# Routing tiles 5 and 6 sorted one by one, weight loads moved ahead of the gather, the last output scattered in two halves

## The chip, the cores and the metric

The kernel runs on one core of a Trainium2 chip. The metric is the device time of one execution in microseconds. A core has five engines that work side by side, each through its own instructions in their order: TensorE (PE in the rows; PEld is its weight loading), VectorE (DVE), ScalarE (ACT), GpSimd (POOL) and SyncE (SP, which here only starts transfers). They wait for each other through semaphores. 16 DMA engines move data between HBM and the on-chip memory.

## The reference

One transformer block over 1024 tokens of width 1024: a modulated norm, an mLSTM mixer beside a dilated attention mixer, an output projection, and then a mixture of experts in which each of 16 experts chooses its 128 tokens. What the change touches is the last part:

```python
def expert_choice_ffn(h, w_router, b_router, w_gate, w_up, w_down):
    cap = (EC_CAPACITY_FACTOR * S) // N_EXPERTS          # 128
    affinity = jax.nn.softmax((h @ w_router + b_router), axis=-1)
    gates, idx = lax.top_k(affinity.transpose(0, 2, 1), cap)
    xin = h[bidx, idx]
    hid = silu(einsum('becd,edf->becf', xin, w_gate)) * einsum('becd,edf->becf', xin, w_up)
    y = einsum('becf,efd->becd', hid, w_down) * gates[..., None]
    return zeros_like(h).at[bidx, idx].add(y)
```

The result is x + gate2 times this. All arithmetic is in f32; the expert weights are 16 experts x 3 matrices of 1024 x 2048 floats, 403 MB.

## The kernel before

The tokens lie in 8 tiles of 128. Three stages matter here.

**The output projection** (`phase_out`) makes the residual stream x tile by tile. Tiles 0 to 2 come together; tiles 3 to 7 follow in a loop of 40 steps (5 tiles x 2 halves x 4 pieces of the contraction), and each step issues three matmuls of 512 columns. A half ends with an addition on VectorE that empties PSUM (line 1196) and a write of x to `out` in HBM. The norm of the tile (`out_norm`), its transposition and its router logits (`out_tail`, line 1150) follow some steps later.

**The routing** needs, for each expert, the 128th largest of 1024 affinities. `route_sort(i0, n)` does softmax for n tiles, transposes the affinities so that experts lie on partitions, takes the 64 largest of each half row in 8 rounds (MAX of eight values, then MATCH_REPLACE, which the trace shows as MATCH_VALUE_LOAD and MATCH_REPLACE8), sorts with a `bitonic` network of 7 levels of two instructions (lines 1285 and 1286), merges the n tiles, and merges the result into `self.best`, the running 128 largest, with 7 more levels. It is a generator: the loop of `phase_out` starts a sort at the steps of the table `SORTS` and lets `pump` advance the oldest sort by `PUMP` pieces in each step. Tiles 0 to 2 are one sort, tiles 3 and 4 one, tiles 5 and 6 one. Tile 7 is sorted in `route_select`, which then makes the threshold `thr` (line 1397), the mask, the slots and a one-hot matrix for expert 0. `route_expert` turns that into row numbers `idx`, and an indirect DMA on GpSimd's queue gathers the 128 rows into `xin` (line 1445).

**The experts** (`phase_experts`) run one after the other. Weights come in pieces of 1 MB into a ring of tiles; `feed` starts a load, `cut_high` makes the rounded part `wh` on ScalarE (line 1489), `cut` makes the rest `wl` on VectorE (line 1505) and feeds the tile again, and `mm` runs the 12 matmuls of a piece, the last four of them on `wl`. `expert_down` for expert e runs while expert e+1 is in work; it ends with two multiplications into `xin` (line 1580) and an indirect DMA that adds the 128 rows into `out` (line 1581), called the scatter here. All scatters add into the same `out`, and in the built program each waits for the scatter ahead of it to land. `idx` tiles come from a set of three buffers (`bufs=3`), so the fourth `idx` takes the buffer of the first when all that read it are done.

Ahead of the gather of expert 0 the first loads are started on SyncE's queue; the last three entries of the list `late` are started on GpSimd's queue behind the gather.

Of the kernel before, what the change touches and what calls it, by code (L numbers as in the profile page):

```python
# [14 lines left out]
I32 = mybir.dt.int32  # L15
AF = mybir.ActivationFunctionType
OP = mybir.AluOpType
# [3 lines left out]
P = 128  # L21
# [23 lines left out]
RING = 8  # L45
EARLY = 6
FEEDS = (2, 8, 14, 20, 26, 32)
LATE = 3
CUTS = 4
HT = (1, 3, 5, 7)  # L50
PAIR0 = 2, 4, 5
MIX = 8
SORTS = {9: (0, 3), 24: (3, 2), 39: (5, 2)}
PUMP = 2
G1 = 3
TAIL1 = 2, 2, 4
TAIL = 4, 6
# [49 lines left out]
class K:  # L107
# [1045 lines left out]
    def phase_out(self):  # L1153
        nc, I, tc, m1, mx = self.nc, self.I, self.tc, self.m1, self.mx
        psum = lambda: self.psm.tile([P, 512], F32, name="pm")
        self.h2_d = tc.dram_tile([S, D], F32, name="h2_d")
        ss = m1.tile([P, 2, NT], F32, name="ss2")
        with ExitStack() as st:
# [34 lines left out]
            def epilogue(i, c, ps):  # L1193

                x, t = X[i][:, c * 512:(c + 1) * 512], slice(c * 512, (c + 1) * 512)
                nc.vector.tensor_add(x, ps, x)
                sq = self.rp.tile([P, 512], BF16, name="sq2", tag="wo_raw", bufs=4)
                nc.scalar.activation(sq, x, AF.Square, accum_out=ss[:, c, i:i + 1])
                nc.sync.dma_start(out=self.out[i * P:(i + 1) * P, t], in_=x)
# [5 lines left out]
            last, spare = psum(), psum()  # L1205
# [23 lines left out]
            todo, side = {}, []  # L1229
            at = lambda n, g: todo.setdefault(n, []).append(g)  # L1230

            def pump(n):
                for _ in range(n):
                    if side and next(side[0], 1):
                        side.pop(0)

            def finish(i, rs, when):
                g = self.out_tail(i, X[i], rs)
                next(g)
                at(when[0], lambda: next(g))  # L1240
                at(when[1], lambda: next(g))
# [8 lines left out]
            for i in range(G1, NT):  # L1250
                for c in range(2):
                    ps = psum()
                    for k in range(MH):
                        mm(ps, i, c, k)
                        step += 1
                        for g in todo.pop(step, ()):
                            g()
                        if step in SORTS:
                            side.append(self.route_sort(*SORTS[step]))
                        if step in FEEDS:  # L1260
                            self.feed()
                        pump(PUMP)
                    epilogue(i, c, ps)
# [30 lines left out]
    def route_sort(self, i0, n, last=False):  # L1294

        nc, rt = self.nc, self.rt
        lg = self.lg[:, i0:i0 + n]
        aff = self.aff[:, i0:i0 + n, 0:NE]
        R = 32 * n
        mx = rt.tile([P, 4], F32, name="r_mx", bufs=2)[:, :n]  # L1300
        sm = rt.tile([P, 4], F32, name="r_sm", bufs=2)[:, :n]
        nc.vector.tensor_reduce(mx, lg, axis=AX.X, op=OP.max)
        nc.vector.tensor_sub(aff, lg, mx[:, :, None].to_broadcast([P, n, NE]))
        if n == 1:
            nc.scalar.activation(aff[:, 0], aff[:, 0], AF.Exp, accum_out=sm)
        else:
            nc.scalar.activation(aff, aff, AF.Exp)
        yield 0
        if n > 1:
            nc.vector.tensor_reduce(sm, aff, axis=AX.X, op=OP.add)  # L1310
        nc.vector.reciprocal(sm, sm)
        nc.vector.tensor_mul(aff, aff, sm[:, :, None].to_broadcast([P, n, NE]))
        ps = self.psm.tile([P, 512], F32, name="pm")
        nc.tensor.transpose(ps[:R, :P], self.aff[:, i0:i0 + n].rearrange("p s e -> p (s e)"), self.ident)

        w = next(self.r_work).rearrange("p (h t) -> p h t", h=2)
        a, b = next(self.bit_a), next(self.bit_b)
        if n > 2:
            y = self.rp.tile([P, P], F32, name="r_rows")
            nc.vector.tensor_copy(y[:R], ps[:R, :P])  # L1320
            yield 0
            t = self.rp.tile([P, 64], F32, name="r_top")
            src = y[:R].rearrange("p (h m) -> p h m", h=2)
            top = a[:R], t[:R]
            w = w[:R]
            for r in range(8):
                for h in range(2):
                    nc.vector.max(top[h][:, 8 * r:8 * r + 8], src[:, h])
                if r < 7:
                    for h in range(2):  # L1330
                        nc.vector.match_replace(w[:, h], top[h][:, 8 * r:8 * r + 8], src[:, h], -1.0)
                    src = w
                yield 0
            nc.vector.tensor_copy(a[:R, 64:], t[:R, ::-1])
        else:

            R2 = slice(0, 2 * R)
            x, w = w[R2, 0], w[R2, 1]
            for h in range(2):
                if last and h == 0:  # L1340
                    nc.vector.tensor_copy(x[h * R:(h + 1) * R], ps[:R, 64 * h:64 * h + 64])
                else:
                    nc.scalar.activation(x[h * R:(h + 1) * R], ps[:R, 64 * h:64 * h + 64], AF.Copy)
            yield 0
            for r in range(8):
                nc.vector.max(a[R2, 8 * r:8 * r + 8], x)
                if r < 7:
                    nc.vector.match_replace(w, a[R2, 8 * r:8 * r + 8], x, -1.0)
                    x = w
                yield 0  # L1350
            nc.vector.tensor_copy(a[:R, 64:], a[R:2 * R, 63::-1])
        yield from self.bitonic(a, b, slice(0, R))
        a, b = self.sorted
        while n > 1:
            R, m = 32 * ((n + 1) // 2), 32 * (n // 2)
            nc.vector.tensor_copy(b[:m], a[R:R + m, ::-1])
            nc.vector.tensor_max(b[:m], a[:m], b[:m])
            if m < R:
                nc.vector.tensor_copy(b[m:R], a[m:R])
            n = R // 32  # L1360
            yield 0
            yield from self.bitonic(b, a, slice(0, R))
            a, b = self.sorted
        if i0:
            nc.vector.tensor_max(b[:32], self.best[:32], a[:32, ::-1])
            if not last:
                yield from self.bitonic(b, a, slice(0, 32))
                a, b = self.sorted
            else:
                a = b  # L1370
        self.best = a
        yield 0
# [137 lines left out]
    def mm(self, xs, n, first, last):  # L1510

        nc = self.nc
        w, l = self.ready.pop(0)
        (xh, xl), ps = xs, n
        N = len(ps) * 512
        prods = (xh, w), (xl, w), (xh, l)
        order = [(q, t, c) for q in range(3) for t in range(FF // N) for c in range(len(ps))]
        if last and not (self.fed or self.halves or self.ready):

            order.sort(key=lambda a: (a[1], a[0], a[2]))  # L1520
        for q, t, c in order:
            x, y = prods[q]
            o = t * N + c * 512
            nc.tensor.matmul(ps[c], x[:, t], y[:, o:o + 512], start=first and q == 0 and t == 0, stop=last and (q, t) == (2, FF // N - 1))  # L1524
        if self.ahead:
            self.ahead -= 1
        else:
            self.cut()
# [36 lines left out]
        self.split(h, l, ps.rearrange("p (k n) -> p k n", k=4))  # L1565
        u.setdefault("hT", []).append((h, l))

    def expert_down(self, u, psum):

        nc = self.nc  # L1570
        ps = [psum() for _ in range(2)]
        for i in range(8):
            h, l = u["hT"][i // 2]
            k = slice(2 * (i % 2), 2 * (i % 2) + 2)
            self.mm((h[:, k], l[:, k]), ps, i == 0, i == 7)
            yield i
        y = self.xin
        for c in range(2):
            t = slice(c * 512, (c + 1) * 512)
            nc.vector.scalar_tensor_tensor(y[:, t], ps[c], u["gate"], self.gate2[:, t], op0=OP.mult, op1=OP.mult)  # L1580
        nc.gpsimd.indirect_dma_start(out=self.out, out_offset=bass.IndirectOffsetOnAxis(ap=u["idx"][:, :1], axis=0),  # L1581
                                     in_=y, in_offset=None, compute_op=OP.add)

    def phase_experts(self):


        nc = self.nc
# [5 lines left out]
        half = lambda pool, tag, **kw: pool.tile([P, D], F32, name="w_half", tag=tag, **kw)  # L1593
        og = lambda: half(self.yp, "og", bufs=MH)
# [2 lines left out]
        self.xin = self.m1.tile([P, D], F32, name="xin", bufs=2)  # L1597
        for _ in range(2):
            self.feed([half(self.yap, "ya", bufs=MH) for _ in range(2)], once=True)
        late = [None] * (RING - EARLY) + [[og(), og()], [og(), half(self.m2, "w_x")]]  # L1600
        for t in late[:-LATE]:
            self.feed(t)
        _, u = self.route_expert(0, sets[1])
        for t in late[-LATE:]:
            self.feed(t, nc.gpsimd)
        for _ in range(CUTS - 1):
            self.cut()
        for b in range(2):
# [4 lines left out]
        p = None  # L1613
        for e in range(NE):
            X, Y = sets[e % 2], sets[1 - e % 2]
            n = None
# [6 lines left out]
            for i in self.expert_up(u, "w_up", Y):  # L1623
# [3 lines left out]
                if e + 1 < NE and i == 2:  # L1627
                    n = next(route)
            for c in range(4):
                t = slice(c * 512, (c + 1) * 512)  # L1630
# [9 lines left out]
                    self.expert_xT(n, b, Y)  # L1640
            p, u = u, n
        self.expert_hT(p, 3, Y)
        for _ in self.expert_down(p, Y):
            pass


# [100 lines left out]
```

## Time and profile before

| | us |
|---|---|
| median of 3 runs | 1841.47 (1836.42 to 1842.91) |
| the profiled execution: time | 1833.95 |
| the profiled execution: span on the core | 1832.0 |
| TensorE busy in that span | 1722.9 (94%) |
| VectorE busy | 1487.1 (81%) |
| ScalarE busy | 1197.7 (65%) |
| time at which the last addition of the projection starts | 640.0 |
| time at which the first expert matmul starts | 679.4 |

Times in the rows below count from the start of the span. The profiled execution is one of its own, 7.5 us below the median of the three runs. Busy shares are means over stages with different limits, so the stages have to be read one by one.

### The profile page before, as it was taken

To read this page: it belongs to the slowest core of one execution; us is meant where nothing else is said; L and a number is where in the kernel's file an instruction comes from. 1 tells how busy PE (TensorE), PEld (TensorE's weight loads), DVE (VectorE), ACT (ScalarE), POOL (GpSimd) and SP (SyncE) were. 2 spreads that over 40 slices of the span, in tenths; PEclk is the share of its full clock that TensorE was granted. 3 is DMA by queue.
4 is the path that set the end of the run, shared out by engine and by line. 5 is a ranking of instruction groups with operands and counts; after the bars stand their busy time and mean duration, and the time that the engine had idled before them with its cause. 6 is when DMAs were issued, how large, how long until landed. Compare 5 with 4: busy or idle time off the path is not lost. (4 is left out here: it accounts for less than half of the span.)

```text
span 1832.0 us, 24429 instructions
## 1 busy us (share of the span) xinstructions
PE 1722.9 (94%) x8696; PEld 1402.8 (77%) x8696; DVE 1487.1 (81%) x2156; ACT 1197.7 (65%) x1603; POOL 180.5 (10%) x185
## 2 busy tenths in 40 slices
PE   5999999989998939999999999999999999999997
PEld 4777888778886827888888778777787777777785
DVE  5578885687866788988988898888898888888886
ACT  5346454377763537787777777776776776777764
POOL 1001000031123020010110000100000001001000
PEclk9999999999999959999999999999999999999999
DMA  9135663325557768999999999999999999999892
GB/s 325 42 114 172 213 215 98 110 80 116 135 129 227 258 255 336 359 354 382 410 363 345 373 345 379 372 335 390 352 369 384 357 364 387 329 382 368 311 391 67
DMA packets 152553, 517.26 MB, mean 282 GB/s; under 512 B 33163, under 2 KB 50833, under 8 KB 116721
## 3 DMA queue, kind: packets, MB, share of 16 engines
q1 hardware_dynamic: 138560, 478.92, 70.7%
q0 software_dynamic: 10960, 36.32, 7.5%
q8 instruction: 68, 1.11, 0.2%
q10 hardware_dynamic: 2912, 0.48, 0.2%
q14 instruction: 53, 0.43, 0.1%
HBM read 488.16 MB, written 27.50 MB: 281 GB/s over the span
## 5 line engine op out<-in xcount | busy, mean ns | idle before, releaser
L1505 DVE TENSOR_TENSOR wl<-w,wh 128x2048 fp32r<-128x2048 f32 x278 | 627.8, 2285 | 81.6 <-ACT wh L1489 81.2
L1489 ACT ACTIVATE wh<-w 128x2048 fp32r<-128x2048 f32 x278 | 523.1, 1919 | 55.2 <-PE py L1524 26.3
L1505 DVE TENSOR_TENSOR wl<-w_half,wh 128x1024 fp32r<-128x1024 f32 x210 | 245.6, 1217 | 8.6 <-ACT wh L1489 8.5
L1489 ACT ACTIVATE wh<-w_half 128x1024 fp32r<-128x1024 f32 x210 | 211.8, 1058 | 24.1 <-PE px L1524 13.1
L1524 PE MATMUL py<-wl,xTh 128*128 128x512 f32 x512 | 139.9, 394 | 7.7 <-DVE wl L1505 7.7
L1524 PE MATMUL px<-wl,xTh 128*128 128x512 f32 x512 | 139.7, 394 | 4.5 <-DVE wl L1505 4.5
L1524 PE MATMUL px<-wh,xTh 128*128 128x512 f32 x512 | 141.1, 395 | 2.3 <-ACT xTh L124 2.1
L1524 PE MATMUL py<-wh,xTh 128*128 128x512 f32 x512 | 140.8, 394 | 2.2 <-ACT wh L1489 2.0
L1524 PE MATMUL py<-wh,xTl 128*128 128x512 f32 x512 | 138.3, 390 | 0.0
L1524 PE MATMUL px<-wh,xTl 128*128 128x512 f32 x512 | 138.1, 391 | 0.0
L1524 PE MATMUL px<-wh,hT 128*128 128x512 f32 x512 | 130.4, 396 | 0.1
L1524 PE MATMUL py<-wh,hT 128*128 128x512 f32 x512 | 129.0, 393 | 0.0
L1524 PEld LDWEIGHTS py<-wl,xTh 128*128 128x128 f32 x512 | 94.6, 188 | 33.4 <-DVE wl L1505 14.6
L1524 PEld LDWEIGHTS px<-wl,xTh 128*128 128x128 f32 x512 | 95.0, 188 | 29.5 <-DVE wl L1505 10.4
L1524 PEld LDWEIGHTS px<-wh,xTh 128*128 128x128 f32 x512 | 95.3, 189 | 23.9 <-ACT xTh L124 2.5
L1524 PEld LDWEIGHTS py<-wh,xTh 128*128 128x128 f32 x512 | 94.7, 188 | 24.0 <-ACT wh L1489 4.5
L1524 PEld LDWEIGHTS px<-wh,hT 128*128 128x128 f32 x512 | 95.6, 190 | 22.1 <-ACT wh L1489 2.1
L1524 PEld LDWEIGHTS px<-wh,xTl 128*128 128x128 f32 x512 | 96.7, 189 | 20.6
L1524 PEld LDWEIGHTS py<-wh,xTl 128*128 128x128 f32 x512 | 96.0, 188 | 20.4 <-DVE xTl L125 0.2
L1524 PEld LDWEIGHTS py<-wh,hT 128*128 128x128 f32 x512 | 95.0, 188 | 20.8 <-ACT wh L1489 0.7
L1581 POOL DMA_INDIRECT out_dram<-xin,idx x16 | 48.3, 3019 | 590.6 <-DVE xin L1580 590.6
L1445 POOL DMA_INDIRECT xin<-h_d,idx x16 | 37.8, 2362 | 477.9 <-DVE rg L1443 197.4
(456 smaller groups left out, 3138.2 us busy)
## 6 DMA issues: line engine op xcount, KB each, us to landing
w<-in_w_down_dram SPq DMA_DIRECT2D x95, 1024.0 KB, 8.4
w<-in_w_gate_dram SPq DMA_DIRECT2D x91, 1024.0 KB, 7.2
w<-in_w_up_dram SPq DMA_DIRECT2D x88, 1024.0 KB, 7.1
w_half<-in_w_gate_dram SPq DMA_DIRECT2D x70, 512.0 KB, 7.6
w_half<-in_w_up_dram SPq DMA_DIRECT2D x70, 512.0 KB, 7.5
w_half<-in_w_down_dram SPq DMA_DIRECT2D x66, 512.0 KB, 8.3
ada_w<-in_w_ada_dram SPq DMA_DIRECT2D x64, 256.0 KB, 3.5
wraw<-in_w_in_dram SPq DMA_DIRECT2D x20, 512.0 KB, 4.3
```

What stands on the lines that cost most here:

```text
L1445: nc.gpsimd.indirect_dma_start(out=xin, out_offset=None, in_=self.h2_d, in_offset=bass.IndirectOffsetOnAxis(ap=idx[:, :1], axis=0))
L1489: act = self.nc.scalar.activation(h[:, j * m:(j + 1) * m], t, AF.Copy)
L1505: self.tc.keep_in_program_order(self.nc.vector.tensor_sub(l[:, c], t, h[:, c]))
L1524: nc.tensor.matmul(ps[c], x[:, t], y[:, o:o + 512], start=first and q == 0 and t == 0, stop=last and (q, t) == (2, FF // N - 1))
L1581: nc.gpsimd.indirect_dma_start(out=self.out, out_offset=bass.IndirectOffsetOnAxis(ap=u["idx"][:, :1], axis=0), in_=y, in_offset=None, comp ...
```

## The change

Four edits. (1) The sort of tiles 5 and 6 together at step 39 becomes a sort of tile 5 at step 31 and one of tile 6 at step 39; `pump` advances up to four pieces per step in place of two; and each sort but that of tile 7 yields 2 four times ahead of the transposition of its affinities, which ends the pumping of that step, so that the transposition comes four steps later in the program. (2) The three late pieces are fed on SyncE's queue ahead of the gather and no longer on GpSimd's behind it. (3) In the very last piece of weights the matmuls are ordered by output half first, so that half 0 is complete after six matmuls and half 1 after twelve. (4) The last expert's output is scattered in two indirect DMAs of half rows; each has row numbers of its own, 2 idx + half, made on VectorE in a tile `row` that is drawn from the `idx` buffers.

```diff
-LATE = 3
-SORTS = {9: (0, 3), 24: (3, 2), 39: (5, 2)}
-PUMP = 2
+SORTS = {9: (0, 3), 24: (3, 2), 31: (5, 1), 39: (6, 1)}
+PUMP = 4
+PAUSE = 4
...
             def pump(n):
                 for _ in range(n):
-                    if side and next(side[0], 1):
+                    r = next(side[0], 1) if side else 2
+                    if r == 1:
                         side.pop(0)
+                    if r == 2:
+                        break
...
         nc.vector.tensor_mul(aff, aff, sm[:, :, None].to_broadcast([P, n, NE]))
+        if not last:
+            for _ in range(PAUSE):
+                yield 2
         ps = self.psm.tile([P, 512], F32, name="pm")
...
         if last and not (self.fed or self.halves or self.ready):
 
-            order.sort(key=lambda a: (a[1], a[0], a[2]))
+            order.sort(key=lambda a: (a[2], a[0], a[1]))
...
-    def expert_down(self, u, psum):
+    def expert_down(self, u, psum, last=False):
...
             nc.vector.scalar_tensor_tensor(y[:, t], ps[c], u["gate"], self.gate2[:, t], op0=OP.mult, op1=OP.mult)
-        nc.gpsimd.indirect_dma_start(out=self.out, out_offset=bass.IndirectOffsetOnAxis(ap=u["idx"][:, :1], axis=0),
-                                     in_=y, in_offset=None, compute_op=OP.add)
+            if last:
+
+                row = self.rt.tile([P, 1], I32, name="idx", bufs=3)
+                nc.vector.tensor_scalar(row, u["idx"], 2.0, float(c), op0=OP.mult, op1=OP.add)
+                nc.gpsimd.indirect_dma_start(out=self.out.rearrange("s (h n) -> (s h) n", h=2), out_offset=bass.IndirectOffsetOnAxis(ap=row[:, :1], axis=0),
+                                             in_=y[:, t], in_offset=None, compute_op=OP.add)
+        if not last:
+            nc.gpsimd.indirect_dma_start(out=self.out, out_offset=bass.IndirectOffsetOnAxis(ap=u["idx"][:, :1], axis=0),
+                                         in_=y, in_offset=None, compute_op=OP.add)
...
-        late = [None] * (RING - EARLY) + [[og(), og()], [og(), half(self.m2, "w_x")]]
-        for t in late[:-LATE]:
+        rest = [None] * (RING - EARLY) + [[og(), og()], [og(), half(self.m2, "w_x")]]
+        for t in rest:
             self.feed(t)
         _, u = self.route_expert(0, sets[1])
-        for t in late[-LATE:]:
-            self.feed(t, nc.gpsimd)
...
-        for _ in self.expert_down(p, Y):
+        for _ in self.expert_down(p, Y, True):
```

How the built programs' instructions stand, at three places. The rows give line, operation, output <- inputs and the shape; lines behind 1230 stand some lines lower in the changed kernel (1285, 1286, 1346, 1397, 1505, 1580, 1581 have become 1288, 1289, 1352, 1403, 1511, 1586, 1594).

The first place is VectorE around the last addition of the projection (`xres`, line 1196). Before:

```order
L1357 TENSOR_TENSOR sort_mem<-sort_mem 32x128
L1285 TENSOR_TENSOR sort_mem<-sort_mem 32x64
L1286 TENSOR_TENSOR sort_mem<-sort_mem 32x64
L1310 TENSOR_REDUCE r_sm<-aff 128x2
L1196 TENSOR_TENSOR xres<-pm,xres 128x512
L1285 TENSOR_TENSOR sort_mem<-sort_mem 32x2x32
L1286 TENSOR_TENSOR sort_mem<-sort_mem 32x2x32
L1311 RECIPROCAL r_sm<-r_sm 128x2
```

In the changed kernel:

```order
L1362 COPY sort_mem<-sort_mem 32x128
L139 SCALAR_TENSOR_TENSOR rs_6490<-n_t,n_y 128x1
L1196 TENSOR_TENSOR xres<-pm,xres 128x512
L1363 TENSOR_TENSOR sort_mem<-sort_mem 32x128
L1150 SCALAR_TENSOR_TENSOR logits<-pm,rs_6490,brow 128x16
L1288 TENSOR_TENSOR sort_mem<-sort_mem 32x64
L1289 TENSOR_TENSOR sort_mem<-sort_mem 32x64
L1305 TENSOR_REDUCE r_mx<-logits 128x1
L1352 MAX sort_mem<-sort_mem 64x8
```

Before, the merge of tiles 3 and 4 is at its third stage there (32x64), and the softmax of tiles 5 and 6 (`r_sm`) is in work. In the changed kernel the merge of tiles 3 and 4 has just begun, and the first round for tile 5 (MAX, 64x8) stands behind the addition. From the row behind this addition to the one that makes `thr`, that one included, VectorE has 140 instructions before and 175 in the changed kernel (a MATCH_REPLACE with its load counted once); ahead of it, from the first row of line 1196 on, 209 and 206.

The second place is VectorE behind the output of expert 13 (line 1580, second half), with the semaphores that each row waits for; DMASW ones are those of GpSimd's transfers. Before:

```order
L1580 SCALAR_TENSOR_TENSOR xin<-px,rg,gate_5119 128x512 [waits PE_49]
L125 TENSOR_TENSOR hT<-px,hT 128x512
L1505 TENSOR_TENSOR wl<-w,wh 128x2048 [waits DMAHW0_49,Activation_49]
L1505 TENSOR_TENSOR wl<-w,wh 128x2048 [waits DMAHW1_49,PE_49,Activation_49]
L1505 TENSOR_TENSOR wl<-w,wh 128x2048 [waits DMAHW2_49,PE_49,Activation_49]
L1505 TENSOR_TENSOR wl<-w,wh 128x2048 [waits DMAHW3_49,PE_49,Activation_49]
```

In the changed kernel:

```order
L1586 SCALAR_TENSOR_TENSOR xin<-px,rg,gate_5119 128x512 [waits PE_49]
L125 TENSOR_TENSOR hT<-px,hT 128x512
L1511 TENSOR_TENSOR wl<-w,wh 128x2048 [waits DMAHW5_49,Activation_49]
L1590 TENSOR_SCALAR idx<-idx 128x1 [waits DMASW7_49]
L1511 TENSOR_TENSOR wl<-w,wh 128x2048 [waits DMAHW6_49,PE_49,Activation_49]
L1511 TENSOR_TENSOR wl<-w,wh 128x2048 [waits DMAHW7_49,PE_49,Activation_49]
L1511 TENSOR_TENSOR wl<-w,wh 128x2048 [waits DMAHW0_49,PE_49,Activation_49]
```

A row of line 1590, the row numbers of the last expert's half 0, now stands behind the first `wl`. Its wait (DMASW7, value 160) is the landing of the scatter of expert 13, which is started by the two multiplications just ahead of it. The same happens a second time, behind the output of expert 14, with the row numbers of half 1, which wait (DMASW0, value 176) for the scatter of expert 14:

```order
L125 TENSOR_TENSOR hT<-px,hT 128x512 [waits Activation_49]
L1511 TENSOR_TENSOR wl<-w,wh 128x2048 [waits DMAHW1_49,Activation_49]
L1590 TENSOR_SCALAR idx<-idx 128x1 [waits DMASW0_49]
L1511 TENSOR_TENSOR wl<-w,wh 128x2048 [waits DMAHW2_49,Activation_49]
L1511 TENSOR_TENSOR wl<-w,wh 128x2048 [waits DMAHW3_49,Activation_49]
L1511 TENSOR_TENSOR wl<-w,wh 128x2048 [waits DMAHW4_49,PE_49,Activation_49]
```

The third place is the end of GpSimd's program. Before:

```order
L1581 DMA out_dram<-xin,idx 1024x1024 [waits DMASW1_49,DVE_49]
L1445 DMA xin<-h_d,idx 128x1024 [waits DMASW2_49,DVE_49,PE_49]
L1581 DMA out_dram<-xin,idx 1024x1024 [waits DMASW3_49,DVE_49]
L1581 DMA out_dram<-xin,idx 1024x1024 [waits DMASW4_49,DVE_49]
L1581 DMA out_dram<-xin,idx 1024x1024 [waits DMASW5_49,DVE_49]
```

In the changed kernel:

```order
L1594 DMA out_dram<-xin,idx 1024x1024 [waits DMASW4_49,DVE_49]
L1451 DMA xin<-h_d,idx 128x1024 [waits DMASW5_49,DVE_49,PE_49]
L1594 DMA out_dram<-xin,idx 1024x1024 [waits DMASW6_49,DVE_49]
L1594 DMA out_dram<-xin,idx 1024x1024 [waits DMASW7_49,DVE_49]
L1591 DMA out_dram<-xin,idx 2048x512 [waits DMASW0_49,DVE_49]
L1591 DMA out_dram<-xin,idx 2048x512 [waits DMASW1_49,DVE_49]
```

The last scatter has become two of half rows, and the second waits for the semaphore that the first one raises on landing (DMASW1), as each scatter before waits for the one ahead of it.

## Rows read from the trace of the kernel before

**Rows 1.** The page: the span of the profiled execution.

```profile
span 1832.0 us, 24429 instructions
```

**Rows 2.** Stretches of 5 us, by engine busy time and count; then granted clock, DMA share, GB/s.

```profile
655.00:660.00 5.00, 0.00 (x0) 0.00 (x0) 4.94 (x38) 2.73 (x2) 0.00 (x0) 0.50 0.62 260
...
665.00:670.00 5.00, 0.69 (x13) 0.47 (x10) 3.99 (x7) 0.00 (x0) 1.52 (x1) 0.50 0.00 0
```

**Rows 3.** TensorE in order of time: start, duration, work, [idle before <- what ended it].

```profile
662.49 0.28 PE L1401 MATMUL pm<-ident,sort_mem 32*128 32x32 f32 x1 [13.05 <-DVE sort_mem L1399]
...
675.34 1.97 PE L1538 MATMUL py<-ident,xin 128*128 128x128 f32 x8 [7.54 <-DMA xin<-h_d,idx]
679.36 2.07 PE L1524 MATMUL px<-wh,xTh 128*128 128x512 f32 x4 [2.05 <-ACT xTh L124]
```

**Rows 4.** VectorE in order of time, between the projection and the routing.

```profile
640.03 0.67 DVE L1196 TENSOR_TENSOR xres<-pm,xres 128x512 f32<-128x512 f32 x1
...
661.68 0.27 DVE L1397 TENSOR_REDUCE thr<-sort_mem 32x1 f32<-32x128 f32 x1
```

**Rows 5.** VectorE in two stretches, ahead of and behind the last addition of line 1196.

```profile
607.00:640.03 33.03, 29.18 (x206) 1.00 0.71 248
640.70:661.68 20.98, 20.28 (x153) 0.62 0.81 300
```

**Rows 6.** VectorE in order of time, around the scatter of expert 13.

```profile
1735.13 0.74 DVE L1580 SCALAR_TENSOR_TENSOR xin<-px,rg,gate 128x512 f32<-128x512 f32 x1
1735.79 0.68 DVE L125 TENSOR_TENSOR hT<-px,hT 128x512 fp32r<-128x512 f32 x1
1736.39 13.29 DVE L1505 TENSOR_TENSOR wl<-w,wh 128x2048 fp32r<-128x2048 f32 x6
```

**Rows 7.** DMA issues from 1735 to 1756 us: queue, count, us to landing.

```profile
out_dram<-xin,idx POOLq DMA_INDIRECT x1, 10.8
```

**Rows 8.** TensorE in order of time, at the same place.

```profile
1739.02 1.07 PE L1524 MATMUL py<-wl,xTh 128*128 128x512 f32 x4
...
1741.74 1.07 PE L1524 MATMUL py<-wl,xTh 128*128 128x512 f32 x4
```

**Rows 9.** GpSimd in order of time: the last three scatters.

```profile
1736.15 1.59 POOL L1581 DMA_INDIRECT out_dram<-xin,idx  x1 [44.07 <-DVE xin L1580]
1799.53 1.57 POOL L1581 DMA_INDIRECT out_dram<-xin,idx  x1 [61.78 <-DVE xin L1580]
1821.31 1.57 POOL L1581 DMA_INDIRECT out_dram<-xin,idx  x1 [20.21 <-DVE xin L1580]
```

**Rows 10.** The chain that ended last, where it passes the scatter of expert 14.

```profile
1799.53 6.17 DMA out_dram<-xin,idx
```

**Rows 11.** VectorE in order of time, from 1795 us to the end.

```profile
1799.77 13.30 DVE L1505 TENSOR_TENSOR wl<-w,wh 128x2048 fp32r<-128x2048 f32 x6
...
1819.44 1.41 DVE L1580 SCALAR_TENSOR_TENSOR xin<-px,rg,gate 128x512 f32<-128x512 f32 x2 [4.11 <-PE px L1524]
```

**Rows 12.** TensorE in order of time, from 1799 us to the end.

```profile
1804.96 1.07 PE L1524 MATMUL px<-wl,hT 128*128 128x512 f32 x4
...
1816.75 1.07 PE L1524 MATMUL px<-wh,hT 128*128 128x512 f32 x4
...
1819.02 0.61 PE L1524 MATMUL px<-wl,hT 128*128 128x512 f32 x2
```

**Rows 13.** Line 1581, the 16 scatters of the whole run.

```profile
DMA to landing us min/median/max: 6.2/11.6/14.6
```

**Rows 14.** The expert stage in 16 stretches of 70 us: their sum.

```profile
sum 1120.00, PE 1098.66 PEld 890.96 DVE 979.03 ACT 825.80 POOL 80.27; mean PE 68.67 PEld 55.69 DVE 61.19 ACT 51.61 POOL 5.02
```

**Rows 15.** SyncE's queue, 680 to 1790 us, waits: us in total, times, longest.

```profile
SPq L1474 <- DVE wl L1505: 634.8, 300, 37.5
```

**Rows 16.** TensorE behind an idle time, and the granted clock of the 3.3 us after it.

```profile
1700.34 1.29 PE L1538 MATMUL py<-ident,xin 128*128 128x128 f32 x5 [2.18 <-DMA xin<-h_d,idx]
```

**Rows 17.** The same place as a stretch: busy time, granted clock, DMA share, GB/s.

```profile
1700.40:1703.70 3.30, 3.30 (x11) 0.50 1.00 359
```


## The prediction

> **What bounds the kernel now.** I read the views from the whole to the single wait: first the page's span (1832.0 us [rows 1]), then stretches of time, then each engine in order of time at the three places that the change touches.
>
> Most of the span is the expert stage. Over its 1120 us TensorE is busy for 1098.66 [rows 14], so it waits 2% of the time. SyncE's loads there wait for VectorE's `wl`, 300 times [rows 15]: a load starts when its tile comes free, so the stream of weights follows the arithmetic and does not lead it. Whatever delays TensorE here comes out at the end in full.
>
> Ahead of it lies a hole. TensorE has finished the projection, stands 13.05 us before it can transpose the threshold, then 7.54 for the gather, and starts the first expert matmul at 679.36 [rows 3]. In the hole VectorE is full (4.94 of 5 us in one stretch [rows 2]): it does the rest of the routing sorts, from the last addition at 640.03 to `thr` at 661.68 [rows 4]. The DMA engines are idle behind that: their share is 0.62 from 655 to 660 us and 0.00 from 665 to 670 [rows 2]. So the hole's length is VectorE's queue, instruction by instruction.
>
> The end of the program is a chain as well: last matmul, two multiplications, scatter, landing.
>
> **Edit 1, the sorts.** Ahead of the last addition VectorE gets about as many instructions as before (206 against 209), so I leave 640.03 where it is; it had 3.85 us of idle time there (33.03 less 29.18 [rows 5]), and the new order doesn't fill it with more. Behind it stand 175 in place of 140 up to `thr`. Tile 5 alone needs all 8 rounds and both networks, and so does tile 6; together they had shared the rounds and one of the merges into `best`. The added 35 are 8 MAX, 7 MATCH_REPLACE, each with its load, and 20 others, mostly of the networks. The stretch of before has 153 instructions, loads included, in 20.98 us [rows 5], 0.137 each. At that price 42 more (35 and 7 loads) cost 5.75 us. The loads are shorter than the mean, so I take **5.5 us**. Bounds: 4.8 when the added work fills gaps between dependent pairs, 7 when ScalarE is late with tile 6 or 7, whose exponentials and copies now stand close together on it. Nothing hides it, as TensorE has no other work in the hole. The pause of four steps removes short waits of TensorE for the transpositions. I cost it at nothing: TensorE has the next steps' matmuls to hide the transposition in, and if that cover failed the cost would be a wait of VectorE's softmax, some tenths of a microsecond, five times.
>
> **Edit 2, the early loads.** Three pieces, 3 MB, now go out on SyncE's queue ahead of the gather, into a time when the DMA engines run dry [rows 2]. The gather itself starts later than before by the 5.5 us, so they are through by then, and its 7.54 us stay. Gain: none that lasts. The ring is full soon after either way, since loads wait for free tiles [rows 15]. Between 1 us of gain (a gather with less beside it) and 1 us of loss I take 0.
>
> **Edit 4, the row numbers.** This is the term that the diff hides. The tile `row` comes from the three `idx` buffers. Half 0 takes the buffer of expert 13, so its instruction on VectorE waits until the scatter of expert 13 has landed. The order puts it behind one `wl` after the multiplications that start that scatter. The scatter starts at 1736.15 [rows 9] and takes 10.8 us to land [rows 7], that is until 1746.95. VectorE, which before ran six `wl` of 2.2 us each in one go from 1736.39 [rows 6], would do one, until 1738.6, and then stand with five behind the waiting instruction. The second `wl` would be done at 1746.95 + 0.15 + 2.29 = 1749.4. TensorE wants it at 1741.74: its groups of four matmuls on `wl` follow at 2.72 us, the first of the six being used at 1739.02 [rows 8]. The stall would be 7.65 us. Landing takes 6.2 us at the least and 14.6 at the most over the 16 scatters [rows 13], which makes 3.1 and 11.5. As no new load is started while VectorE stands, the scatter should meet somewhat less traffic: I take **6.6 us**. Afterwards VectorE gains only 0.5 us per piece on TensorE, and the stage has no idle time in which to make it good.
>
> Half 1 takes the buffer of expert 14. That scatter starts at 1799.53 [rows 9] and lands 6.17 us later, at 1805.70 [rows 10], with hardly a load left beside it. VectorE runs one `wl` from 1799.77 to about 1802.0 [rows 11], then waits; its second is done at 1805.70 + 0.15 + 2.29 = 1808.1, where TensorE wants it at 1804.96 [rows 12]. **3.2 us**, between 2.9 and 3.5, as the conditions are those of before.
>
> An idle time on TensorE can cost twice. Behind one of 2.18 us [rows 16] the granted clock was 0.50 for the next 3.3 us [rows 17], the 1.2 GHz level, and half of that time, 1.65 us, was lost. For the two new stalls I take **1.7 us** together, between 0 and 3.4.
>
> **Edits 3 and 4, the end.** Before, the last 12 matmuls start at 1816.75, both halves are ready near 1819.5, and the scatter starts at 1821.31 [rows 9, 11, 12]. Now half 0 is ready six matmuls earlier (0.227 us each, 1.36) and doesn't wait for the second multiplication (0.7): its scatter starts 2.0 us earlier. But the scatter of half 1 waits for it to land. No row shows a scatter of 256 KB. The nearest is the 512 KB at 6.17 [rows 10]. If a half cost as much, the end would come at -2.0 + 6.2 = 4.2 us later; if it cost half as much, 1.1 us later. Two halves that each take 4 to 5.2 us give +0 to +2.2 against the one of 6.2. I take **2.0 us**, as the start of the transfer and the semaphore at its end aren't halved, and 0 to 4.2 as bounds.
>
> The Trainium skill (DMA: Bandwidth & Descriptors, Anatomy of one DMA — SWDGE (gpsimd) path) gives about 2.0 us per transfer plus its bytes at 436 GB/s, so an estimate of 3.2 us for the whole and 2.6 for each half: by that estimate the end would be no later at all (-2.0 - 3.2 + 5.2 = 0). The row with 6.17 us for a whole one stands against its 3.2.
>
> **The sum**, against the profiled execution (1833.95 us): 5.5 + 0 + 6.6 + 3.2 + 1.7 + 2.0 = 19.0, so 1853. That execution lies 7.5 us under the median of the three runs (1841.47). The forecast for a median of runs is therefore 1841.5 + 19.0 = 1860.5, 1.0% slower. A change under 0.5% (9.2 us) can't be told from none with a kernel whose runs spread like this.
>
> **Rivals.**
>
> *The scatters land fast.* With VectorE held, loads stop, and the scatter of expert 13 might land in the 6.2 us of [rows 13], as that of expert 14 does without traffic. Then 3.1 replaces 6.6 and the clock doesn't fall: 5.5 + 3.1 + 3.2 + 0 to 1 = 12 to 13, 1854. Against it: the loads already under way at 1738.6 are not recalled, and one scatter with full traffic beside it took 10.8 [rows 7].
>
> *Tile 5 leaves the tail.* If the sort of tile 5 were through before the last addition, 45 instructions and 7 loads (7.1 us at 0.137) would go from the tail, 5.5 would turn into -1.6, and with fast scatters the sum would be 6 to 7, 1848, within the bound. The Trainium skill (Trace Analysis, Optimizing Scalar/DVE Operations) says that breaking up instructions may let work finish sooner where VectorE is not saturated. In the hole it is saturated by [rows 2], and the order shows tile 5's first round behind the addition.
>
> *Weights were the limit.* If the expert stage were bound by its stream of weights, the 3 MB started in dead time would shorten it by 3.1 MB / (403 MB in 1140 us), 8.9 us. The later start and the stalls of VectorE would be covered by the stream, and the time would be 1841.5 - 8.9 + 2.0 = 1835, faster by 0.4%, or by 0.5% and more if the end costs nothing. It decides if loads and not `wl` are what TensorE waits for. Against it: the loads wait for VectorE [rows 15], and TensorE is busy 98% [rows 14].
>
> **How the numbers follow.** The forecast gets 0.78, fast scatters 0.11, tile 5 out of the tail 0.06, the stream 0.05. Predicted is 1860. The low bounds of all terms (4.8 - 1 + 3.1 + 2.9) give about 10, or 1851; the high ones (7 + 1 + 11.5 + 3.5 + 3.4 + 4.2) 30, or 1871. With some 3 us for where the three runs fall, and without the unlikely corner of all high bounds together, 1848 to 1871 holds 8 in 10. Slower by over 0.5% are the forecast and most of the fast scatters: 0.87. Within 0.5%: 0.09. Faster: 0.04.
>
> **What would show it.** In the changed kernel's trace: some 5 us more between the last line 1196 and `thr`, and the first expert matmul that much later; on VectorE two instructions of line 1590 whose idle time before them ends by a DMA into `out_dram`, about 8 us behind expert 13's output and 3.6 behind expert 14's; behind each, TensorE waiting for `wl` for 3 to 8 us; two scatters of line 1591 with the second starting only when the first has landed. It would be wrong if line 1590 waited for nothing long, or if the stage between the two stalls ran faster than before.

## The result and the profile after

The changed kernel takes 1858.97 us, the median of 4 runs (1857.64 to 1864.22), against 1840.11 for the kernel before in the same session (4 runs, 1836.42 to 1842.91). The ratio is 1.0109, with a 95% interval of 1.0081 to 1.0137: about 20 us slower. The prediction was 1860 us.

The profiled execution of the changed kernel has this span (the page), which answers to [rows 1] and is 23.7 us longer:

```profile
span 1855.7 us, 24481 instructions
```

The reading goes in the order of time. First VectorE between the projection and the routing; the two rows answer to [rows 4]:

```profile
642.92 0.69 DVE L1196 TENSOR_TENSOR xres<-pm,xres 128x512 f32<-128x512 f32 x1 [0.62 <-PE pm L1185]
...
669.58 0.27 DVE L1403 TENSOR_REDUCE thr<-sort_mem 32x1 f32<-32x128 f32 x1
```

The last addition starts 2.9 us later than before, and from it to `thr` pass 26.66 us in place of 21.65. TensorE in the same hole (start, duration, work, idle time before it and what ended that), to set beside [rows 3]:

```profile
670.30 0.31 PE L1407 MATMUL pm<-ident,sort_mem 32*128 32x32 f32 x1 [11.44 <-DVE sort_mem L1405]
...
682.86 1.94 PE L1544 MATMUL py<-ident,xin 128*128 128x128 f32 x8 [7.23 <-DMA xin<-h_d,idx]
```

The wait for the gather is as long as it was (7.23 against 7.54). The first expert matmul starts at 686.88, 7.5 us later than before: 2.9 from ahead of the addition, 5.0 from the sorts, 0.4 less behind them.

Then VectorE behind the outputs of experts 13 and 14, beside [rows 6, 11]:

```profile
1741.33 0.75 DVE L1586 SCALAR_TENSOR_TENSOR xin<-px,rg,gate 128x512 f32<-128x512 f32 x1
...
1742.59 2.28 DVE L1511 TENSOR_TENSOR wl<-w,wh 128x2048 fp32r<-128x2048 f32 x1
1752.92 0.15 DVE L1590 TENSOR_SCALAR idx<-idx 128x1 int32<-128x1 int32 x1 [8.05 <-DMA out_dram<-xin,idx]
1753.03 11.10 DVE L1511 TENSOR_TENSOR wl<-w,wh 128x2048 fp32r<-128x2048 f32 x5
...
1816.03 2.28 DVE L1511 TENSOR_TENSOR wl<-w,wh 128x2048 fp32r<-128x2048 f32 x1
1821.87 0.15 DVE L1590 TENSOR_SCALAR idx<-idx 128x1 int32<-128x1 int32 x1 [3.56 <-DMA out_dram<-xin,idx]
1821.95 11.10 DVE L1511 TENSOR_TENSOR wl<-w,wh 128x2048 fp32r<-128x2048 f32 x5
```

Where VectorE made six `wl` in one go, it now makes one, stands 8.05 and 3.56 us until a DMA into `out_dram` has landed, does 0.15 us of work on the row numbers, and makes the other five. TensorE shows the same two holes a little later:

```profile
1755.38 2.08 PE L1530 MATMUL py<-wl,xTh 128*128 128x512 f32 x4 [7.27 <-DVE wl L1511]
...
1824.30 1.19 PE L1530 MATMUL px<-wl,hT 128*128 128x512 f32 x4 [2.92 <-DVE wl L1511]
```

The first group of four took 2.08 us, where the same group took 1.07 before [rows 8]. Stretches of the trace (busy time and count of PE, PEld, DVE, ACT, POOL; then the granted clock, the DMA share and GB/s) say why:

```profile
1750.50:1760.70 10.20, 5.32 (x13) 4.17 (x14) 7.78 (x5) 1.91 (x1) 0.00 (x0) 0.50 0.64 235
1760.70:1771.00 10.30, 10.30 (x47) 8.54 (x46) 5.79 (x4) 5.48 (x7) 0.00 (x0) 1.00 0.98 381
1819.00:1825.60 6.60, 3.68 (x17) 2.72 (x16) 3.73 (x3) 5.46 (x4) 0.00 (x0) 1.00 0.31 60
1825.60:1829.00 3.40, 3.40 (x10) 2.62 (x9) 3.40 (x3) 0.90 (x2) 0.00 (x0) 0.50 0.00 0
```

The clock was granted at 0.50, the 1.2 GHz level, for all of the 5.32 us that TensorE worked behind the first stall, and for 3.40 us behind the second, where it fell only after 1.30 us of work (1824.30 to 1825.60). A group of four takes twice as long at that level, so half of such time is lost: 2.66 and 1.70 us.

The end, on GpSimd's queue, beside [rows 9]:

```profile
1742.36 1.58 POOL L1594 DMA_INDIRECT out_dram<-xin,idx  x1 [42.06 <-DVE xin L1586]
1815.80 1.56 POOL L1594 DMA_INDIRECT out_dram<-xin,idx  x1 [71.86 <-DVE xin L1586]
1840.88 1.55 POOL L1591 DMA_INDIRECT out_dram<-xin,idx  x1 [23.53 <-DVE xin L1586]
1846.56 1.54 POOL L1591 DMA_INDIRECT out_dram<-xin,idx  x1 [4.12 <-DMA out_dram<-xin,idx]
```

The second half scatter starts 5.68 us behind the first, and its idle time ends by a DMA into `out_dram`. The chain that ended last runs through the scatter of expert 14, the `wl` behind it, and the first half scatter:

```profile
1815.80 6.05 DMA out_dram<-xin,idx
1821.95 2.31 DVE wl L1511
1824.30 15.53 PE px L1530 x60
1839.85 0.76 DVE xin L1586
1840.62 0.27 issue
1840.88 4.92 DMA out_dram<-xin,idx
```

From the last matmul's end to the end of the span it is 15.0 us, before 12.4. TensorE's last twelve matmuls, beside [rows 12]:

```profile
1837.84 1.07 PE L1530 MATMUL px<-wh,hT 128*128 128x512 f32 x4
1838.74 0.39 PE L1530 MATMUL px<-wl,hT 128*128 128x512 f32 x1
1838.97 0.61 PE L1530 MATMUL px<-wh,hT 128*128 128x512 f32 x2
1839.42 0.39 PE L1530 MATMUL px<-wl,hT 128*128 128x512 f32 x1
1839.65 0.61 PE L1530 MATMUL px<-wh,hT 128*128 128x512 f32 x2
1840.11 0.61 PE L1530 MATMUL px<-wl,hT 128*128 128x512 f32 x2
```

The first multiplication into `xin` starts at 1839.85, as the eighth of the twelve ends. So half 0 is complete after eight matmuls, where the order in the source has it complete after six.

### The profile page after: what moved, and what is told of

Read it like the earlier page. It is cut to its first block, busy times and chain, and to the rows that moved or that the text cites. A ratio compares the mean times of both kernels' runs of the same rounds, so it can differ in the third digit from the quotient of the medians.

```text
span 1855.7 us, 24481 instructions
## 1 busy us (share of the span) xinstructions
PE 1729.3 (93%) x8697; PEld 1406.8 (76%) x8697; DVE 1489.0 (80%) x2197; ACT 1198.6 (65%) x1608; POOL 180.3 (10%) x181
## 5 line engine op out<-in xcount | busy, mean ns | idle before, releaser
L1511 DVE TENSOR_TENSOR wl<-w_half,wh 128x1024 fp32r<-128x1024 f32 x210 | 245.8, 1219 | 10.3 <-ACT wh L1495 10.3
L1530 PEld LDWEIGHTS px<-wl,xTh 128*128 128x128 f32 x512 | 95.3, 189 | 29.7 <-DVE wl L1511 10.5
L1530 PEld LDWEIGHTS py<-wh,xTl 128*128 128x128 f32 x512 | 96.5, 189 | 20.8 <-DVE xTl L125 0.2
```

Of the source, the lines that this page charges most:

```text
L1511: self.tc.keep_in_program_order(self.nc.vector.tensor_sub(l[:, c], t, h[:, c]))
```

## The experiments

Theory A, tested here, is the prediction's: the loss is the sum of three separate costs, the two waits of the row numbers with the half-speed stretches behind them, the added instructions of the sorts, and the second half scatter at the end. The main rival B is that the stage makes the stalls good, so that sorts and end carry the loss; the others stand with the expectations. Eleven kernels were run. Because the part ahead of the routing starts and ends at varying times (last section), the profiled executions are compared by stretches: A from the last addition of line 1196 to `thr`, B from `thr` to the first expert matmul, C from that to the end of the last matmul, D from there to the end of the span. The ratio is that of the times to the kernel before in the same session, with its 95% interval.

| kernel | ratio | A | B | C | D |
|---|---|---|---|---|---|
| before | 1 | 21.65 | 17.68 | 1140.27 | 12.37 |
| changed | 1.0109 (1.0081 to 1.0137) | 26.66 | 17.30 | 1153.84 | 14.98 |
| e1_bufs4 | 1.0083 (1.0067 to 1.0098) | 26.63 | 17.66 | 1149.06 | 14.96 |
| e2_wholeout | 1.0012 (1.0002 to 1.0021) | 26.65 | 17.74 | 1141.13 | 11.41 |
| e3_sorts | 1.0027 (1.0016 to 1.0038) | 26.64 | 17.51 | 1141.28 | 12.37 |
| e4_loads | 1.0005 (0.9992 to 1.0017) | 21.64 | 17.66 | 1138.06 | 12.03 |
| e5_halves | 1.0099 (1.0084 to 1.0114) | 21.66 | 17.51 | 1155.31 | 15.38 |
| e6_halves4 | 1.0067 (1.0050 to 1.0084) | 21.65 | 17.52 | 1148.62 | 15.19 |
| e7_pump | 0.9988 (0.9979 to 0.9998) | 22.75 | 15.77 | 1139.46 | 12.42 |
| e8_split2 | 1.0039 (1.0026 to 1.0051) | 26.46 | 17.45 | 1138.69 | 12.47 |
| e10_bufs5 | 1.0040 (1.0027 to 1.0053) | 26.66 | 17.49 | 1138.31 | 15.04 |
| e11_halves5 | 1.0017 (1.0008 to 1.0026) | 21.66 | 17.47 | 1140.79 | 15.16 |
| e12_best | 0.9988 (0.9975 to 1.0001) | 22.75 | 15.77 | 1140.65 | 11.47 |

Where nothing stalls, C lies between 1138.06 and 1141.28 (nine kernels, mean 1139.8), so a difference in C under 3 us tells nothing.

**e1_bufs4**: the changed kernel with four `idx` buffers.

```diff
-        idx = rt.tile([P, 1], I32, name="idx", bufs=3)
+        idx = rt.tile([P, 1], I32, name="idx", bufs=4)
...
-                row = self.rt.tile([P, 1], I32, name="idx", bufs=3)
+                row = self.rt.tile([P, 1], I32, name="idx", bufs=4)
```

> The changed kernel with four idx buffers in place of three, all else kept; the row numbers then take buffers whose readers are long done. Theory A (the row numbers' waits cost in full): the two waits of line 1590 (8.05 and 3.56 us) and TensorE's two waits for wl behind them (7.3 and 2.9 us) go, and with them the half-speed stretches (2.65 and 1.7 us), so 14 to 15 us less than the changed kernel: 1844 to 1845. Rival B (the stage makes the stalls good, since the ring is full of loads when VectorE goes on): 0 to 3 us less, 1856 to 1859.

Measured 1853.06 us, which is what neither theory gave. Its line 1590 on VectorE shows why:

```profile
1699.98 0.14 DVE L1590 TENSOR_SCALAR idx<-idx 128x1 int32<-128x1 int32 x1
...
1756.41 0.15 DVE L1590 TENSOR_SCALAR idx<-idx 128x1 int32<-128x1 int32 x1 [8.17 <-DMA out_dram<-xin,idx]
```

I had been wrong about what the edit does. With four buffers half 0 takes the buffer of expert 12 and moves 50 us forward, but half 1 now takes that of expert 13 and stands where half 0 stood, with the same wait of 8 us. Only the second stall went: C fell by 4.8 us, and the second stall with its half-speed stretch was 2.92 + 1.70 = 4.6. TensorE still shows the first one:

```profile
1758.87 2.07 PE L1530 MATMUL py<-wl,xTh 128*128 128x512 f32 x4 [7.36 <-DVE wl L1511]
```

**e10_bufs5**: the same with five buffers, made to settle what e1 left open.

```diff
-        idx = rt.tile([P, 1], I32, name="idx", bufs=3)
+        idx = rt.tile([P, 1], I32, name="idx", bufs=5)
...
-                row = self.rt.tile([P, 1], I32, name="idx", bufs=3)
+                row = self.rt.tile([P, 1], I32, name="idx", bufs=5)
```

> The changed kernel with five idx buffers. With four, the row numbers of half 0 took the buffer of expert 12 and those of half 1 that of expert 13, so one of the two waits (8.2 us, for the scatter of expert 13) stayed. With five both take buffers of scatters that have landed long before. Theory A (each wait costs its stall and the half-speed stretch behind it): the stage from the first expert matmul to the last loses 7.4 + 2.6 = 10 us more and comes to 1139 to 1141 us, the time to 1843 to 1845. Rival B (with no wait left, something else of the half scatters still costs in the stage): the stage stays above 1145, the time near 1850.

Measured 1844.78 us, with C at 1138.31, a bit below what theory A gave. The view of line 1590 has both instructions at 1699.1 and names no idle time of the engine ahead of them:

```profile
L1590 DVE TENSOR_SCALAR idx<-idx x2: 145/145/145, 1699.1 to 1699.1; 128x1 int32<-128x1 int32 x2
its engine sat idle before it (us, times) until:
who waited for it (us, times):
```

So the two waits carry 15.5 us of C (14.0 against the mean of the nine kernels without stalls), and the size of one small buffer set is the whole cause of them: the computation, its instructions and its transfers are those of the changed kernel.

**e2_wholeout**: the changed kernel with the last output scattered whole; the last matmuls stay in the order by halves.

```diff
-        for _ in self.expert_down(p, Y, True):
+        for _ in self.expert_down(p, Y):
```

> The changed kernel with the last output scattered whole, the order of the last matmuls by halves kept; sorts and loads kept. Theory A: the waits for row numbers go (14 to 15 us) and the end's second scatter too (2.6 us), and the first multiplication now lies beside the last six matmuls (0.7 us): 1859 - 18 = 1841, 3 us below the kernel with four buffers. Rival B (stalls made good): only the end gains, 1855 to 1856. Rival C (half scatters cost nothing at the end, by the estimate from the Trainium skill's figures): the same as with four buffers.

Measured 1839.64 us, 0.12% above before. No wait is left, as no row numbers are made, and D is 11.41, 3.6 us less than in e10, which keeps the half scatters. The ratios of the two differ by 0.28%, 5 us. Theory A's 3 us is borne out to within what the intervals tell, and rival C (halves that cost nothing) is out. The whole scatter on GpSimd:

```profile
1828.37 1.55 POOL L1594 DMA_INDIRECT out_dram<-xin,idx  x1 [19.59 <-DVE xin L1586]
```

It starts 1.08 us behind the last matmul's end (1827.29), where the kernel before took 1.68: the order by halves puts the first multiplication beside the last matmuls. From this scatter's start to the end of the span are 10.3 us.

**e3_sorts**: the kernel before with edit 1 alone.

```diff
-SORTS = {9: (0, 3), 24: (3, 2), 39: (5, 2)}
-PUMP = 2
+SORTS = {9: (0, 3), 24: (3, 2), 31: (5, 1), 39: (6, 1)}
+PUMP = 4
+PAUSE = 4
```

(with the changed `pump` and the yields of `route_sort`, as in the change)

> The kernel before with edit 1 alone: tiles 5 and 6 sorted singly, four pieces a step, the transposition four steps later. Theory A: about 5 us more between the last addition of the projection and the threshold, and that much in the time: 1845. Rival B (the row numbers don't cost, the sorts and what follows from them carry nearly all): 1852 to 1856. Rival D (the early loads hide the longer hole and only without them does it show more): above 1847.

Measured 1843.05 us, 0.27% or 5.0 us above before, and A is the changed kernel's. It is below rival B's 1852 and rival D's 1847, so neither of the two holds here. VectorE (lines stand one lower here):

```profile
645.20 0.69 DVE L1197 TENSOR_TENSOR xres<-pm,xres 128x512 f32<-128x512 f32 x1 [0.63 <-PE pm L1186]
...
671.84 0.27 DVE L1404 TENSOR_REDUCE thr<-sort_mem 32x1 f32<-32x128 f32 x1
```

**e8_split2** and **e7_pump** take edit 1 apart: the split of the sort without the pause and with two pieces a step, and the pause and four pieces without the split.

```diff
-SORTS = {9: (0, 3), 24: (3, 2), 39: (5, 2)}
+SORTS = {9: (0, 3), 24: (3, 2), 31: (5, 1), 39: (6, 1)}
```

That is e8_split2 against the kernel before, and this is e7_pump against e3_sorts:

```diff
-SORTS = {9: (0, 3), 24: (3, 2), 31: (5, 1), 39: (6, 1)}
+SORTS = {9: (0, 3), 24: (3, 2), 39: (5, 2)}
```

> The kernel before with tiles 5 and 6 sorted singly, but two pieces a step and no pause. Theory A (the added instructions cost, wherever they stand): 5 to 7 us more, 1845 to 1847. Rival G (the pause and the pump carry the cost): 0 to 1 us more, 1840 to 1841.

> The kernel before with four pieces a step and the transposition four steps later, but tiles 5 and 6 still sorted as one. Theory A (the added instructions cost): as many instructions as before, so 0 to 2 us more, 1840 to 1842. Rival G (the later transposition pushes work behind the last addition, and the split is harmless): about 5 us more, 1845.

The split alone cost 7.2 us (1.0039 of 1837), 4.8 of it in A; the interval takes in the 5 us of e3. The other half alone made the kernel 0.12% faster, just told apart from no change. So the added instructions cost, and rival G, which gave the whole 5 us to the pause and the pump, falls. But e7 shows something that theory A had not. A is 1.1 us longer: as the transposition comes later, VectorE has 160 instructions in that stretch, where the kernel before has 153 [rows 5]. And B is 1.9 us shorter. The gather's row on GpSimd and the `wl` beside it on VectorE, in e7:

```profile
672.25 1.05 POOL L1452 DMA_INDIRECT xin<-h_d,idx  x1 [4.98 <-DVE rg L1450]
672.55 6.69 DVE L1512 TENSOR_TENSOR wl<-w,wh 128x2048 fp32r<-128x2048 f32 x3 [0.40 <-issue]
```

The same two in the kernel before:

```profile
668.43 6.70 DVE L1505 TENSOR_TENSOR wl<-w,wh 128x2048 fp32r<-128x2048 f32 x3
668.48 3.17 POOL L1445 DMA_INDIRECT xin<-h_d,idx  x1 [4.98 <-DVE rg L1443]
```

The gather's instruction took 1.05 us on GpSimd, where it took 3.17 in the kernel before and in the changed one. Before, VectorE had begun a `wl` 0.05 us ahead of it; in e7 the `wl` begins 0.30 us behind it. The first of the three `wl` ends at 668.43 + 2.23 = 670.66, and 1.05 us after that is 671.71, where the gather's instruction ends (668.48 + 3.17 = 671.65). So the longer time is that of an instruction that stands until that `wl` is done, as far as the rows tell; no run changes this order alone.

**e4_loads**: the kernel before with edit 2 alone.

```diff
-        for t in late[:-LATE]:
+        for t in rest:
             self.feed(t)
         _, u = self.route_expert(0, sets[1])
-        for t in late[-LATE:]:
-            self.feed(t, nc.gpsimd)
```

> The kernel before with edit 2 alone: the late pieces fed on SyncE's queue ahead of the gather. Theory A: 0, between 1 us less and 1 us more, 1839 to 1841, with the gather's wait of 7.5 us kept. Rival E (the stream of weights is the limit of the expert stage): 3 MB ahead of it give up to 8.9 us, 1831 to 1834. Rival F (SyncE's queue holds the gather's neighbours up): a gather wait longer by 1 us or more.

Measured 1838.32 against 1837.78 us: no difference that can be told. The gather's wait is 7.52, so rival F is out. C is 1138.06, 2.2 us less than before; but over the kernels without stalls it is 1139.5 on average for four with the early loads (e2, e4, e10, e12) and 1140.1 for five without (before, e3, e7, e8, e11), so the 8.9 us of rival E are excluded.

**e5_halves**, **e6_halves4** and **e11_halves5**: the kernel before with edits 3 and 4, with three, four and five `idx` buffers.

```diff
-            order.sort(key=lambda a: (a[1], a[0], a[2]))
+            order.sort(key=lambda a: (a[2], a[0], a[1]))
...
+                row = self.rt.tile([P, 1], I32, name="idx", bufs=3)
```

(with the rest of the changed `expert_down`; 4 and 5 in place of 3 in both places of the other two)

> The kernel before with edits 3 and 4 alone: last matmuls by halves, two half scatters with row numbers drawn from the three idx buffers. Theory A: both waits of line 1590 and the longer end without the sorts: 14 to 15 + 2.6 = 17 us more, 1857. Rival B (stalls made good): 1842 to 1845.

> The kernel before with edits 3 and 4 and four idx buffers: what the half scatters do at the end, without the waits for buffers. Theory A: 2 to 3 us more than the kernel before, 1842 to 1843, with 15 us from the last matmul's end to the end of the span in place of 12.4. Rival C (two halves cost no more than one whole): 1840 and a stretch of at most 12.5 us.

> The kernel before with edits 3 and 4 and five idx buffers: the half scatters alone with neither wait. Theory A: only the end is longer, 15.2 us from the last matmul in place of 12.4, so 2 to 3.5 us above the kernel before. Rival H (matmuls by halves or the half scatters cost in the stage as well): 6 us or more above it, as with four buffers (11).

With three buffers 1855.79 us, 0.99% above before; with four 1848.34, 0.67%; with five 1840.29, 0.17%. The stalls of the first are the changed kernel's, on VectorE:

```profile
1748.95 0.15 DVE L1584 TENSOR_SCALAR idx<-idx 128x1 int32<-128x1 int32 x1 [8.38 <-DMA out_dram<-xin,idx]
...
1818.28 0.15 DVE L1584 TENSOR_SCALAR idx<-idx 128x1 int32<-128x1 int32 x1 [3.49 <-DMA out_dram<-xin,idx]
```

With four, one stays, as in e1, which the expectation had missed in the same way (11 us where 2 to 3 were expected). With five only the end is longer, by 2.8 us in D, as theory A said, and rival H falls. The steps in C agree with e1 and e10 from the other side: one stall costs 8.8 us (1148.62 less 1139.8), both 15.5.

**e12_best**: the parts that cost nothing, together: e7_pump, the early loads, and the last matmuls by halves with one whole scatter.

```diff
-PUMP = 2
+PUMP = 4
+PAUSE = 4
...
-        for t in late[:-LATE]:
+        for t in rest:
...
-            order.sort(key=lambda a: (a[1], a[0], a[2]))
+            order.sort(key=lambda a: (a[2], a[0], a[1]))
```

> The kernel before with what cost nothing of the change: four pieces a step and the later transposition with tiles 5 and 6 still sorted as one, the early loads, and the last matmuls by halves with one whole scatter. Theory A (the parts add up): 0.5 to 1 us less from the last addition to the first expert matmul, 1 us less at the end, 0 to 2 us from the loads: 1.5 to 4 us below the kernel before, 0.1 to 0.2%. Rival: the parts share one gain and 0 to 1 us is left.

Measured 1835.15 against 1837.14 us; the interval (0.9975 to 1.0001) doesn't part it from the kernel before. Its trace has the parts, 0.8 us less in A and B and 0.9 less in D. They are too small to show in the time.

## Why the prediction was right

The mechanisms were those of the prediction; the sizes were off in places, and part of that cancelled.

- **Edit 1.** Forecast 5.5 us, measured 5.0 in A, with and without the other edits. The count was right: the stretch from the addition to `thr` holds 196 instructions in place of 153, 43 more where I had 42. The mean of [rows 5] made 5.75 us of them, 15% too much. As A is longer, the rival in which tile 5 leaves the tail is out. That the pause costs nothing holds within 0.2 us with the sorts split (26.66 with it, 26.46 without); with the joint sort it added 1.1 us to A (e7).
- **Edit 2.** Forecast 0, measured 0.9 us with an interval of -1.5 to 3.1.
- **Edit 4, the row numbers.** Forecast 6.6 and 3.2, measured 7.27 and 2.92 as idle time of TensorE. The scatter of expert 13 took 10.5 us to land (it starts at 1742.36, and VectorE goes on at 1752.92), nearly the 10.8 of [rows 7]. The discount that I took, that it would meet less traffic with VectorE held, was the wrong part of the step; without it the row's own working gave 7.65. So the rival of fast scatters, whose condition was a landing in 6.2 us, doesn't hold either. Its sum also lacked the 2.0 us of the end, and its premise that the clock stays up behind a stall of 3 us fails too: it fell behind the one of 2.92.
- **The clock** is the term that I mis-sized: "For the two new stalls I take 1.7 us together, between 0 and 3.4". It was 2.66 + 1.70 = 4.4, above my bound. I had carried over the 3.3 us at half speed of [rows 17], which follow an idle time of 2.18 us. Behind 7.27 us of idle time the next 5.32 us of work were at half speed, and the second stall alone cost as much as I gave to both. These 4.4 us are read from the trace; no run undoes the clock without the stall.
- **The end.** Forecast 2.0, measured 2.6. Half 0 started 0.16 us behind the last matmul's end in place of 1.68, a gain of 1.5 and not 2.0. The step that failed there is that half 0 is ready six matmuls earlier: it is ready after eight of the twelve, and the first multiplication starts 0.87 us ahead of the last matmul's end, where before it was 0.19 [rows 11, 12]. That is 0.7 us earlier and not 1.36. The second started 5.68 us later. From its start to the end of the span are 9.1 us, against 10.7 for the whole one before. -1.5 + 5.7 - 1.6 = 2.6. The measured landing of a half, 4.92, lies between the two cases that I had bounded it with. One of these I had summed wrongly: two halves that took half as long each would have ended the program 2.0 us earlier (-2.0 + 2 x 3.1 - 6.2) and not 1.1 later. The 2.0 that I took doesn't hang on it, but the low bound of 0 should have been -2.

The Trainium skill (DMA: Bandwidth & Descriptors, Anatomy of one DMA — SWDGE (gpsimd) path) gives about 2.0 us per transfer plus its bytes at 436 GB/s, and the estimate from that would have made the halves free at the end. The trace disagrees: 4.92 us for 256 KB where that estimate is 2.6.

In the profiled pair the stretches give 5.0 - 0.4 + 13.6 + 2.6 = 20.8 us, and the other 2.9 of the 23.7 lie ahead of the last addition. C grew by 13.6 where stalls and clock add up to 14.6, within what C varies by itself. Undone on the chip, the waits are worth 0.69% (changed less e10) to 0.82% (e5 less e11), 13 to 15 us; forecast were 11.5 with the clock. The edits measured in three groups (e3, e4 and e5: 0.27, 0.05 and 0.99%) add up to 1.31%, a little more than the 1.09% of all together, which the intervals of both allow. That 1860 came within 1 us of the median is luck to some extent: the clock was 2.7 too small, and the kernel before ran 1.4 us faster in the session of the result than in the runs that the forecast started from.

## What to carry to other kernels

A small tile drawn from an existing buffer set inherits the waits of whatever used that buffer last: look up which instruction frees it, how long that one takes, and what stands behind the new instruction on its in-order engine. One buffer more may only hand the wait to the next user; count the tiles until the wait falls on work that is long done, here five where three stood. A transfer split to start earlier pays its fixed part twice when the second part must wait for the first. What two halves cost that don't wait for each other was not tried.

## What had not been expected of the hardware

- Two sizes of the accumulating scatter with little traffic beside them landed in 5.97 to 6.31 us (512 KB: the scatter of expert 14, shortest in e2 and longest in e8; [rows 10] has 6.17) and in 4.69 to 4.92 us (256 KB: the first half, shortest in e11). If the time is a fixed part and one by size, an estimate from these two sizes makes the fixed part 3.1 to 3.9 us.
- The length of the half-speed stretch differed. It was 5.32 us of work behind an idle time of 7.27, with the clock already at 0.50 when the work began, and 3.40 behind one of 2.92, where the first 1.30 us of work still ran at 1.00. In e1_bufs4, behind 7.36 us, the second group of four matmuls already took 1.65 us and the third 1.09.
- The gather's instruction held GpSimd for 3.16 or 3.17 us in eleven kernels and for 1.05 in the two with the pause and the joint sort (e7, e12), where the gather also landed sooner (4.5 and 4.4 us against 6.8 before). GpSimd stood as long ahead of it (4.98 us). What goes with the difference in all thirteen traces is the order: in the eleven a `wl` on VectorE had begun 0.05 us earlier, in the two it began 0.30 us later. It was not tried by itself.
- The last addition of the projection starts between 640.0 and 647.1 us in the profiled executions. Both ends belong to kernels (before and e11) with the same program up to there, so a span by itself doesn't tell a few us.
